# Eighteen assumed latencies of the mixers' streams raised in the driver that orders TensorE's work

## The chip, the cores and the metric

The kernel runs on one core of one Trainium2 chip. The metric is the device time of one execution in microseconds, as the median of several runs; a profiled execution beside them gives the trace. TensorE multiplies matrices, VectorE (DVE), ScalarE (ACT) and GpSimd (POOL) work on elements, SyncE (SP) issues the DMAs. The engines run side by side and wait for each other through semaphores. Each takes its own instructions in order.

## What is computed

A decoder block on 16 learned meta tokens and 512 tokens of width 1024: three token mixers in parallel, a gated merge, and a convolutional feed-forward net.

```python
h = rmsnorm(z)
p = h @ w_in                                  # 1024 x 8464: GLA, HGRN2, gates, RWKV-7
y_gla, y_hg = chunked gated linear attention  # chunks of 32, a state per head
y_rw = RWKV-7: S_t = S_{t-1} (diag(w_t) - kk_t^T (a_t kk_t)) + v_t^T k_t
z = z + (sum of sigmoid(gate_b) * (y_b @ w_out_b)) @ w_out
u = rmsnorm(z) @ w_up
z = z + (silu(conv(u)[:, :2816]) * conv(u)[:, 2816:]) @ w_down
return rmsnorm(z)[16:]
```

## The kernel before

The big products (GEMMs) are made in float16 with a high and a low part of both operands, three matmuls for one, and read their weights from HBM in blocks of 128 columns: a DMA brings a block (`wf`), ScalarE makes the high part and VectorE the low part (`split_w`, L202 and L203, tile `w`). Each such block is an *item*: 48 matmuls for a block of 1024 rows, 24 for one of 512. The items before the feed-forward net are the columns of `w_in` (one for each of q, k, v, f, g of a head or a pair of heads, and 24 gates) and the products with `w_out_*`. An item ends with the evacuation of its PSUM bank (`then`).

The mixers work on these columns in *streams*, Python generators: in the first drive four HGRN2 heads (`hg0` to `hg3`) and two pairs of GLA heads (`gl0`, `gl1`), index 0 to 5; in the second drive RWKV-7, four pairs of heads in `rw_phase1`, then the inversion of the chunks' triangular matrices on VectorE and GpSimd (`invert`, L1194 and L1199), then four pairs in `rw_phase2`. The steps of a stream are small matmuls and transposes in float32, named by their PSUM tile:

- `lin_mixer`: `pk`, `pmt`, `pv` transpose k and v; `ps0` and `pin` make the states; `pc` the scores; `po` and `pom` the outputs; `pt` transposes them back.
- `rw_phase1`: `psu`, `psa` (low rank parts), `pss` and `prb`, `prm` (norm of kk and its broadcast), `pM`, `pMm` (the matrices that are inverted).
- `rw_phase2`: `pQ`, `pN`, `tA`, `tB`, `tK`, `tV`, `tm`, `psb`, `psx`, then, with the inverse, `p1`, `p2`, `pw`, `ph`, `pf`, then the chain over eight chunks (`pc`, with latency `ch` between two chunks), and `pyt`.

Each `yield latency, banks` in a stream tells the driver how long after the step before it the next one's operands are expected, and how many of the four small PSUM banks must be free by its own account. The latencies stand in the table `LT`. `drive` fixes TensorE's order by hand when the kernel is built: it keeps a modelled clock `pe.t` (`Paced`), takes a step of a stream as soon as the clock has passed its due time, enough banks are counted free and the stream owes no filler (`owed`: after a step some filler, 0.7 of its time), and otherwise issues matmuls of the items, the *filler*. It is the order alone that is fixed so; on the chip each matmul waits for its operands. The other engines' order is made by the scheduler of the framework.

Gates: a stream can yield a name and waits for that event (`at(name, latency)`); an item can too, and then holds all items behind it. The f item of HGRN2 head 2 waits for `hg0`, the end of head 0's stream; the k item of RWKV pair 2 waits for `a0`, the end of pair 0's phase 1, that of pair 3 for `a1`. `T`, the inverse, is assumed 53.8 us after `a3`. Phase 2 of a pair waits for the r item of that pair, and that of pair 3 for `y0`, the end of pair 0. The chunk chains wait for `out27`, the end of the last product of HGRN2's output. The last items before the merge (`rw_item`) need `y0` to `y3`; the first of them takes three of its k blocks for two output blocks (36 of 48 matmuls) ahead of `y3`.

Of the kernel before, what the change touches and what calls it, by code (L numbers as in the profile page):

```python
# [18 lines left out]
P = 128  # L19
# [4 lines left out]
T = NMETA + SEQ  # L24
# [24 lines left out]
LT = dict(  # L49
    f=17.0, pk=(1.0, 1.89, 0.0, 0.0, 1.0, 0.0), pv=0.0, ps0=1.2, pc=0.75,  # L50
    po=(4.08, 2.75, 0.98, 0.0, 0.0, 2.0), pt=(10.56, 10.58, 9.41, 18.52, 18.27, 9.18), gk=0.75, v=0.0,
    gv=4.09, k=4.31, pss=(1.14, 1.4, 0.28, 1.69), prb=(2.37, 3.25, 2.02, 2.9),
    pM=(2.7, 3.05, 4.48, 2.95), pMm=0.0, r=18.93, rv=0.9, g=1.82, T=53.8, pN=0.0, tA=2.44, tB=0.0, tK=0.8,
    tm=3.44, psb=1.1, psx=1.06, p1=11.9, p2=3.06, pw=5.19, ph=0.44, pf=0.1, ch0=0.0, ch=3.4, gn=3.11, y=9.68,
    hold=1.85, mix=0.7,
)
# [38 lines left out]
def trunk(ctx: ExitStack, tc: tile.TileContext, d: dict, out: bass.AP):  # L95
# [143 lines left out]
    with tc.tile_pool(name="xin", bufs=1, side="right") as xp:  # L239
# [13 lines left out]
        pt = bank("mix_ps", P, KD)  # L253
# [111 lines left out]
    pt = bank("par_ps", P, npar)  # L365
# [216 lines left out]
    def lin_mixer(im, gev, nm, gsum, gscale, q, k, vs, sgs, normw, ys):  # L582
# [52 lines left out]
        pk = bank(f"pk{nm}", P, 4, P)  # L635
# [11 lines left out]
        for h in range(nh):  # L647
            yield LT["pv"], 1
            pv = bank(f"pv{nm}{h}", P, 4, P)
            for t in range(4):  # L650
                pe.transpose(pv[:, t, :], vs[h][:, 16 + P * t : 16 + P * (t + 1)], ident)
            v_ = lt.tile([P, 4, P], F32, tag=f"vt{h}", name=f"vt{nm}{h}")
            act.activation(v_, pv, AF.Copy)
            vt.append(v_)


        S = lt.tile([P, 4, P], F32, tag="S", name=f"S{nm}")
        yield LT["ps0"], 2
        ps0 = bank(f"ps0{nm}", P, P)
# [11 lines left out]

        yield LT["pc"], 2
        stv = []
# [3 lines left out]
        pcs = [bank(f"pc{nm}{h}", P, 4, P) for h in range(nh)]  # L677
# [333 lines left out]
    def rw_phase1(i):  # L1011
# [95 lines left out]
        for h, pq in enumerate(pqs):  # L1107
            vec.tensor_copy(Mt[:, :, h, :], pq)
        yield LT["pMm"], 2
        pms = [bank(f"pMm{i}{h}", 16, 16) for h in range(2)]  # L1110
# [119 lines left out]
    def rw_phase2(i, r1, E0, ANs, Xs, HVs, s2, s2m, s3):  # L1230
# [58 lines left out]
        for h, (pq, hr) in enumerate(zip(pqs, hrs)):  # L1289
            for q, (rr, sr_) in enumerate(par):  # L1290
                vec.tensor_tensor(X[rr, :, h, rr], pq[rr, 4 * q : 4 * q + 4, :], mU[rr], op=ALU.mult)
                vec.tensor_tensor(E[sr_, q:8:2, h, rr], pq[sr_, 4 * q : 4 * q + 4, :], mU[sr_], op=ALU.mult)
        yield LT["pN"], 2
        pns = [bank(f"pN{i}{h}", P, 4, 64) for h in range(2)]
# [7 lines left out]
        for h, (pn, hr) in enumerate(zip(pns, hrs)):  # L1302
            for q, (rr, sr_) in enumerate(par):
                vec.tensor_tensor(AN[rr, :, h, sr_], pn[rr], mL[rr], op=ALU.mult)
        yield LT["tA"], 1
        pa = tok4(f"tA{i}", Ap, 0)
# [3 lines left out]
        for h, hr in enumerate(hrs):  # L1310
            for q, (rr, sr_) in enumerate(par):
# [116 lines left out]
        yield LT["ch0"], 1

# [383 lines left out]
```

## Time and profile before

| | us |
|---|---|
| median of 3 runs | 1027.21 |
| lowest and highest run | 1023.19, 1027.33 |
| the profiled execution | 1026.22 |
| span of the profiled execution, first to last instruction | 1023.9 |

| stretch of the span, us | what runs |
|---|---|
| 0 to 250.7 | prologue, and drive 1: HGRN2 and GLA streams among their items |
| 250.7 to 324.1 | phase 1 of RWKV-7 |
| 324.1 to 443 | inversion, and phase 2 of pairs 0 to 2 up to the chunk chains |
| 443 to 578.3 | chunk chains of all pairs, phase 2 of pair 3 |
| 578.3 to 615.3 | last gates and products of RWKV-7's output |
| 615.3 to 1023.9 | product with `w_out`, feed-forward net, final norm |

In the profile PE is TensorE's matmuls and PEld its weight loads. A wait is idle time of an engine that a semaphore ended; the name behind the arrow is who set it. PEclk is the clock that TensorE was granted, as a share of 2.4 GHz; 0.50 is 1.2 GHz. A row of a window gives its bounds and length, the busy time of PE, PEld, DVE, ACT and POOL with their counts of instructions, PEclk, the busy share of the DMA engines, and GB/s. `g` is the PSUM tile of the GEMMs, `g<-hT,w` a matmul of an item of `w_in`, `g<-y,w` one of `w_out_*`. The names of tiles leave numbers out, so that `pinhg` is `pin` of an HGRN2 head and `pM` that of any pair.

### The profile page before, as it was taken

How to read it: one execution, taken by the hardware profiler on the slowest of the kernel's cores; microseconds unless marked ns; L12 is line 12 of the kernel's file. 1: busy time of each engine (PE TensorE's matmuls, PEld its weight loads, DVE VectorE, ACT ScalarE, POOL GpSimd, SP SyncE). 2: the span in 40 equal slices, each digit the busy share in tenths (PEclk: the TensorE clock that was granted, in tenths of full speed). 3: DMA queues.
4: the chain of work that ended last, by engine and by line, in shares of the span. 5: the costliest groups of instructions: out<-in, count | busy, mean ns of one | idle time of the engine just before them, and what ended most of it. 6: DMA issues, size and time to landing. Idle time of an engine off the chain costs nothing.

```text
span 1023.9 us, 20898 instructions
## 1 busy us (share of the span) xinstructions
PE 984.7 (96%) x8694; PEld 775.6 (76%) x8694; DVE 638.2 (62%) x1234; ACT 467.1 (46%) x882; POOL 140.4 (14%) x307
## 2 busy tenths in 40 slices
PE   8999989999999989999999989999999999999996
PEld 7888877887778868788878874488888888854442
DVE  5677655445677998677644485567777677783211
ACT  6767565435654444344433353553334443552100
POOL 3122211201333511111000123000000000000100
PEclk9999999999999999999999999999999999999999
DMA  6322222233224314122233463023333333472100
GB/s 192 106 69 58 63 63 83 63 94 81 84 70 115 91 46 126 39 67 63 59 87 84 126 226 106 1 84 104 104 92 96 102 104 104 146 229 99 42 14 28
DMA packets 149289, 92.35 MB, mean 90 GB/s; under 512 B 17664, under 2 KB 142073, under 8 KB 149195
## 3 DMA queue, kind: packets, MB, share of 16 engines
q1 hardware_dynamic: 149195, 91.02, 31.3%
q8 instruction: 68, 1.11, 0.5%
q14 instruction: 26, 0.21, 0.1%
HBM read 86.92 MB, written 3.95 MB: 89 GB/s over the span
## 4 chain that ended last, share of the span: by engine, by line
PE 72%; DVE 12%; ACT 7%; DMA 3%; issue 3%; POOL 2%; SPq 0%; POOLq 0%; DVEq 0%; ACTq 0%
PE g L70 56%; PE dn L70 6%; DVE w L203 2%; DVE AN L1199 1%; DVE HV L1194 1%; DMA wf<-in_w_out_dram 1%; PE pc L70 1%; ACT w L202 1%; PE pf L70 1%; PE hT L75 1%; PE pw L70 1%; PE pogl L70 1%; ACT L383 1%; DMA z<-in_x_dram 1%; PE pcgl L70 0%
## 5 line engine op out<-in xcount | busy, mean ns | idle before, releaser
L70 PEld LDWEIGHTS <-w 128*128 128x128 f16 x5856 | 570.2, 99 | 89.4 <-issue 9.2
L70 PE MATMUL g<-hT,w 128*128 128x256 f16 (+3 forms) x5280 | 620.5, 274 | 2.6 <-ACT siluhg L383 2.2
L203 DVE SCALAR_TENSOR_TENSOR w<-wf,w 128x1024 f16<-128x1024 f32 (+1 forms) x131 | 150.7, 1151 | 93.8 <-ACT w L202 93.5
L202 ACT ACTIVATE w<-wf 128x1024 f16<-128x1024 f32 (+1 forms) x131 | 130.6, 999 | 108.0 <-PE g L70 96.1
L70 PEld LDWEIGHTS <-hid 128*128 128x128 f16 x528 | 51.7, 98 | 63.0 <-issue 1.1
L70 PE MATMUL g<-y,w 128*128 128x258 f16 x576 | 75.3, 273 | 3.5 <-DVE y L447 2.0
L1691 DVE SCALAR_TENSOR_TENSOR c<-u,parB,c 128x512 f32<-128x512 f32 x88 | 66.1, 751 | 2.4
L70 PE MATMUL g<-wd,hid 128*128 128x512 f16 x264 | 57.3, 379 | 0.8 <-DVE z L1742 0.8
L70 PE MATMUL dn<-wd,hid 128*128 128x512 f16 x264 | 57.1, 379 | 0.0
L1746 POOL TENSOR_SCALAR ssf<-ssf 128x1 f32<-128x1 f32 x4 | 2.2, 540 | 311.2 <-ACT sq L1744 311.1
L70 PE MATMUL g<-woh,mT 128*128 128x512 f16 x128 | 38.9, 379 | 0.6 <-DVE z L1645 0.6
L1709 ACT ACTIVATE c<-c 128x512 f32<-128x512 f32 x22 | 13.9, 630 | 53.8 <-DVE c L1691 53.8
L1744 ACT ACTIVATE sq<-z 128x512 f32<-128x512 f32 x8 | 5.0, 628 | 72.3 <-DVE z L1742 72.3
L70 PEld LDWEIGHTS <-mT 128*128 128x128 f16 x192 | 18.5, 98 | 24.2 <-issue 2.9
L1725 DVE SCALAR_TENSOR_TENSOR wd<-wf,wd 128x1024 f16<-128x1024 f32 x22 | 26.9, 1224 | 15.6 <-ACT wd L1724 15.4
L1724 ACT ACTIVATE wd<-wf 128x1024 f16<-128x1024 f32 x22 | 23.3, 1057 | 25.1 <-DMA wf<-in_w_down_dram 25.1
L1443 POOL TENSOR_TENSOR gv<-gv,mhalf 128x2 f32<-128x2 f32 (+1 forms) x16 | 13.9, 876 | 136.2 <-DVE gv L1442 136.2
L1742 DVE SCALAR_TENSOR_TENSOR z<-g,z 128x512 f32<-128x512 f32 x4 | 2.8, 692 | 45.8 <-PE g L70 45.8
L383 ACT ACTIVATE u<-g 128x258 f32<-128x258 f32 x88 | 29.2, 373 | 0.0
L1474 ACT ACTIVATE HV<-pc 64x128 f32<-64x128 f32 x32 | 8.4, 272 | 42.8 <-DVE HV L1473 39.4
L70 PE MATMUL g<-wol,mT 128*128 128x512 f16 x64 | 24.3, 379 | 0.0
L1689 DVE TENSOR_SCALAR c<-u,parB 128x512 f32<-128x512 f32 x44 | 23.8, 542 | 0.0
(484 smaller groups left out, 1195.6 us busy)
## 6 DMA issues: line engine op xcount, KB each, us to landing
wf<-in_w_in_dram SPq DMA_DIRECT2D x65, 512.0 KB
wf<-in_w_up_dram SPq DMA_DIRECT2D x44, 512.0 KB
wf<-in_w_down_dram SPq DMA_DIRECT2D x22, 512.0 KB
wf<-in_w_out_dram SPq DMA_DIRECT2D x8, 512.0 KB
xt<-in_x_dram SPq DMA_DIRECT2D x4, 512.0 KB
wf<-in_w_out_hg_dram SPq DMA_DIRECT2D x8, 256.0 KB
wf<-in_w_out_gla_dram SPq DMA_DIRECT2D x8, 256.0 KB
wf<-in_w_out_rw_dram SPq DMA_DIRECT2D x8, 256.0 KB
```

Source lines behind the costliest of these rows:

```text
L70: r = self.eng.matmul(out, lhsT=lhsT, rhs=rhs, **kw)
L75: r = self.eng.transpose(out, in_, ident)
L202: act.activation(wh[:, :kt, :m], wf[:, :kt, :m], AF.Copy, scale=WS)
L203: vec.scalar_tensor_tensor(wl[:, :kt, :m], wf[:, :kt, :m], WS, wh[:, :kt, :m], ALU.mult, ALU.subtract)
L383: act.activation(dst[:m, off + c0 : off + c0 + n], src, func, **kw)
L1194: eng.tensor_tensor(u, bc(mats[:, j, j + 1 : n], c1 - c0), Ti[:, j, c0:c1].unsqueeze(1).broadcast_to([cnt, r, c1 - c0]), op=ALU.mult)
L1443: gps.tensor_tensor(var, var, mhalf[:, 0 : 2 * n].rearrange("p (a b) -> p a b", b=2), op=ALU.pow)
L1689: vec.tensor_scalar(c, u[:, 0:SEQ], colB(52 + j), colB(8 + j), ALU.mult, ALU.add)
L1691: vec.scalar_tensor_tensor(c, u[:, t : t + SEQ], colB(52 + 44 * t + j), c, ALU.mult, ALU.add)
L1709: act.activation(cg, cg, AF.Silu)
L1724: act.activation(wd[f][:, 0], wf, AF.Copy, scale=WS)
L1725: vec.scalar_tensor_tensor(wd[f][:, 1], wf, WS, wd[f][:, 0], ALU.mult, ALU.subtract)
```

## The change

The entries of `LT` that were one number for all heads or pairs become tuples with a number for each, and the `yield`s read them by index (`[im]` in `lin_mixer`, `[i]` in RWKV-7). Eighteen of the numbers are raised; the others stay. Nothing else changes: no instruction is added or taken away, the order in which `drive` puts them is made anew from the table. The diff, with the raised entries and two of the yields:

```diff
 LT = dict(
-    f=17.0, pk=(1.0, 1.89, 0.0, 0.0, 1.0, 0.0), pv=0.0, ps0=1.2, pc=0.75,
-    po=(4.08, 2.75, 0.98, 0.0, 0.0, 2.0), pt=(10.56, 10.58, 9.41, 18.52, 18.27, 9.18), gk=0.75, v=0.0,
-    gv=4.09, k=4.31, pss=(1.14, 1.4, 0.28, 1.69), prb=(2.37, 3.25, 2.02, 2.9),
-    pM=(2.7, 3.05, 4.48, 2.95), pMm=0.0, r=18.93, rv=0.9, g=1.82, T=53.8, pN=0.0, tA=2.44, tB=0.0, tK=0.8,
-    tm=3.44, psb=1.1, psx=1.06, p1=11.9, p2=3.06, pw=5.19, ph=0.44, pf=0.1, ch0=0.0, ch=3.4, gn=3.11, y=9.68,
-    hold=1.85, mix=0.7,
+    pk=(2.6, 1.89, 0.0, 0.0, 1.0, 0.0),
...
+    ps0=(1.2, 1.87, 1.2, 1.2, 3.96, 1.58),
+    pc=(0.75, 0.75, 0.75, 0.75, 1.57, 0.75),
+    po=(4.08, 2.75, 0.98, 1.7, 0.0, 2.0),
...
+    pss=(2.38, 1.4, 0.28, 1.69),
+    prb=(4.27, 4.12, 3.18, 3.37),
...
+    tA=(5.4, 3.11, 2.44, 2.44),
...
+    tK=(0.8, 1.29, 0.8, 0.8),
...
+    psb=(3.13, 1.1, 1.1, 1.1),
+    psx=(1.06, 1.06, 1.63, 1.06),
...
+    pw=(5.19, 6.5, 5.19, 5.19),
...
+    ch=(3.4, 3.4, 4.02, 3.4),
...
-        yield LT["ps0"], 2
+        yield LT["ps0"][im], 2
...
-                yield LT["ch"], 0
+                yield LT["ch"][i], 0
```

`ch` also sets how long the bank of the chunk chain is counted as taken, `hold=8 * (LT["ch"][i] + 0.5)`.

## Rows read from the trace of the kernel before

**Rows 1.** The page: engines' busy us; costliest groups; one window (core, engines' busy, PEclk).

```profile
PE 984.7 (96%) x8694; PEld 775.6 (76%) x8694; DVE 638.2 (62%) x1234; ACT 467.1 (46%) x882; POOL 140.4 (14%) x307
...
L203 DVE SCALAR_TENSOR_TENSOR w<-wf,w 128x1024 f16<-128x1024 f32 (+1 forms) x131 | 150.7, 1151 | 93.8 <-ACT w L202 93.5
...
443.00:578.30 135.30, 132.36 (x1381) 115.64 (x1380) 79.75 (x207) 54.24 (x126) 14.14 (x17) 1.00 0.27 74
```

**Rows 2.** Waits of TensorE: line waited for: us in total, times, longest.

```profile
PE tA L75 <- issue: 2.7, 1, 2.7
...
PE pingl L70 <- ACT vtgl L653: 2.5, 1, 2.5
...
PE psb L70 <- DVE Nm L1351: 1.8, 1, 1.8
...
PE pohg L70 <- DVE st L697: 1.5, 1, 1.5
...
PE prm L75 <- POOL rnm L1072: 1.4, 3, 0.6
...
PE pkhg L75 <- DVE k6hg L622: 1.4, 1, 1.4
...
PE pss L70 <- issue: 1.0, 1, 1.0
...
PE prb L75 <- ACT rnx L1069: 1.0, 1, 1.0
...
PE prb L75 <- DVE Mt L1108: 0.9, 1, 0.9
...
PE pw L70 <- ACT AN L1308: 0.8, 1, 0.8
...
PE ps0hg L70 <- DVE mthg L645: 0.4, 1, 0.4
...
PE tA L75 <- DVE ARBK L1292: 0.4, 1, 0.4
```

**Rows 3.** Windows after two waits, and one of 40 us: engines' busy, PEclk, DMA.

```profile
178.03:184.18 6.15, 6.15 (x38) 4.55 (x38) 2.05 (x6) 4.76 (x6) 1.15 (x7) 0.50 0.32 88
...
365.34:368.50 3.16, 3.16 (x15) 2.45 (x16) 3.06 (x9) 1.64 (x3) 0.00 (x0) 0.50 0.07 22
...
330.00:370.00 40.00, 37.28 (x359) 31.89 (x357) 39.66 (x112) 18.07 (x42) 20.33 (x44) 0.96 0.32 88
```

**Rows 4.** Timeline, VectorE and TensorE, at gate `hg0`: start, us, instruction.

```profile
70.13 0.82 DVE L729 TENSOR_TENSOR ohg<-ohg,rshg 128x640 f32<-128x640 f32 x1
...
74.48 0.66 PE L75 MATMUL pthg<-ident,ohg 128*128 128x128 f32 x4
```

**Rows 5.** Timeline, TensorE, before gate `a0`.

```profile
269.31 0.61 PE L70 MATMUL g<-hT,w 128*128 128x272 f16 x4
...
272.08 0.23 PE L75 MATMUL prm<-ident,rnm 16*128 16x16 f32 x1 [0.50 <-POOL rnm L1072]
...
272.24 2.87 PE L70 MATMUL g<-hT,w 128*128 128x272 f16 x24
...
275.05 0.69 PE L70 MATMUL pM<-ARBK 64*64 64x64 f32 x32
...
275.67 1.41 PE L70 MATMUL g<-hT,w 128*128 128x272 f16 x11
...
277.02 0.22 PE L70 MATMUL pMm<-ARBK,BKm 64*16 64x16 f32 x4
```

**Rows 6.** Timeline, the DMA queue and TensorE, at the inverse's load.

```profile
389.83 1.81 SPq L1369 DMA_DIRECT2D TT<-s  x4
...
396.77 0.60 PE L70 MATMUL p<-TT,Mt 32*32 32x32 f32 x26
```

**Rows 7.** Timeline, VectorE and TensorE, at the end of the streams.

```profile
581.88 0.42 DVE L1460 TENSOR_TENSOR y<-ARBK,y 128x256 f16<-128x256 f32 x1
...
584.16 5.49 PE L70 MATMUL g<-y,w 128*128 128x258 f16 x48
```

More of the change, by code (lines that the diff above doesn't have):

```diff
@@ L49 @@
 LT = dict(
-    f=17.0, pk=(1.0, 1.89, 0.0, 0.0, 1.0, 0.0), pv=0.0, ps0=1.2, pc=0.75,
-    po=(4.08, 2.75, 0.98, 0.0, 0.0, 2.0), pt=(10.56, 10.58, 9.41, 18.52, 18.27, 9.18), gk=0.75, v=0.0,
-    gv=4.09, k=4.31, pss=(1.14, 1.4, 0.28, 1.69), prb=(2.37, 3.25, 2.02, 2.9),
-    pM=(2.7, 3.05, 4.48, 2.95), pMm=0.0, r=18.93, rv=0.9, g=1.82, T=53.8, pN=0.0, tA=2.44, tB=0.0, tK=0.8,
-    tm=3.44, psb=1.1, psx=1.06, p1=11.9, p2=3.06, pw=5.19, ph=0.44, pf=0.1, ch0=0.0, ch=3.4, gn=3.11, y=9.68,
-    hold=1.85, mix=0.7,
+    f=17.0,
+    pk=(2.6, 1.89, 0.0, 0.0, 1.0, 0.0),
+    pv=(0.0, 0.0, 0.0, 0.0, 0.0, 0.0),
+    ps0=(1.2, 1.87, 1.2, 1.2, 3.96, 1.58),
+    pc=(0.75, 0.75, 0.75, 0.75, 1.57, 0.75),
+    po=(4.08, 2.75, 0.98, 1.7, 0.0, 2.0),
+    pt=(10.56, 10.58, 9.41, 18.52, 18.27, 9.18),
+    gk=0.75,
+    v=0.0,
+    gv=4.09,
+    k=4.31,
+    pss=(2.38, 1.4, 0.28, 1.69),
+    prb=(4.27, 4.12, 3.18, 3.37),
+    pM=(2.7, 3.05, 4.48, 2.95),
+    pMm=(0.0, 0.0, 0.0, 0.0),
+    r=18.93,
+    rv=0.9,
+    g=1.82,
+    T=53.8,
+    pN=(0.0, 0.0, 0.0, 0.0),
+    tA=(5.4, 3.11, 2.44, 2.44),
+    tB=(0.0, 0.0, 0.0, 0.0),
+    tK=(0.8, 1.29, 0.8, 0.8),
+    tm=(3.44, 3.44, 3.44, 3.44),
+    psb=(3.13, 1.1, 1.1, 1.1),
+    psx=(1.06, 1.06, 1.63, 1.06),
+    p1=(11.9, 11.9, 11.9, 11.9),
+    p2=(3.06, 3.06, 3.06, 3.06),
+    pw=(5.19, 6.5, 5.19, 5.19),
+    ph=(0.44, 0.44, 0.44, 0.44),
+    pf=(0.1, 0.1, 0.1, 0.1),
+    ch0=(0.0, 0.0, 0.0, 0.0),
+    ch=(3.4, 3.4, 4.02, 3.4),
+    gn=(3.11, 3.11, 3.11, 3.11),
+    y=9.68,
+    hold=1.85,
+    mix=0.7,
 )
@@ L647, in lin_mixer @@
         for h in range(nh):
-            yield LT["pv"], 1
+            yield LT["pv"][im], 1
             pv = bank(f"pv{nm}{h}", P, 4, P)
@@ L669, in lin_mixer @@
             vec.scalar_tensor_tensor(S[:, t + 1], S[:, t], DT[:, t : t + 1], pin[:, t, :], ALU.mult, ALU.add)
-        yield LT["pc"], 2
+        yield LT["pc"][im], 2
         stv = []
@@ L1108, in rw_phase1 @@
             vec.tensor_copy(Mt[:, :, h, :], pq)
-        yield LT["pMm"], 2
+        yield LT["pMm"][i], 2
         pms = [bank(f"pMm{i}{h}", 16, 16) for h in range(2)]
@@ L1292, in rw_phase2 @@
                 vec.tensor_tensor(E[sr_, q:8:2, h, rr], pq[sr_, 4 * q : 4 * q + 4, :], mU[sr_], op=ALU.mult)
-        yield LT["pN"], 2
+        yield LT["pN"][i], 2
         pns = [bank(f"pN{i}{h}", P, 4, 64) for h in range(2)]
@@ L1304, in rw_phase2 @@
                 vec.tensor_tensor(AN[rr, :, h, sr_], pn[rr], mL[rr], op=ALU.mult)
-        yield LT["tA"], 1
+        yield LT["tA"][i], 1
         pa = tok4(f"tA{i}", Ap, 0)
@@ L1315, in rw_phase2 @@
                 )
-        yield LT["tB"], 1
+        yield LT["tB"][i], 1
         pb = tok4(f"tB{i}", Bd, 16)
@@ L1319, in rw_phase2 @@
             act.activation(X[rr, :, :, kc], pb[rr], AF.Copy)
-        yield LT["tK"], 1
+        yield LT["tK"][i], 1
         pk = tok4(f"tK{i}", Kd, 16)
@@ L1332, in rw_phase2 @@
             act.activation(HV[sr_, q:8:2, :, :], pv[sr_], AF.Copy)
-        yield LT["tm"], 2
+        yield LT["tm"][i], 2
         pm = bank(f"tm{i}", 16, 3, P)
@@ L1351, in rw_phase2 @@
             vec.tensor_tensor(Nm[:, h, :], pm[:, 4:20], maskL[0:16, 0:16], op=ALU.mult)
-        yield LT["psb"], 2
+        yield LT["psb"][i], 2
         rw_bonus(i)
         yield "g"
-        yield LT["psx"], 2
+        yield LT["psx"][i], 2
         lg = sv[:, 0:NY]
@@ L1373, in rw_phase2 @@
         sp.dma_start(TTm, s2m[2 * i : 2 * i + 2].rearrange("h i c -> i h c"))
-        yield LT["p1"], 2
+        yield LT["p1"][i], 2
         p1 = bank(f"p1_{i}", P, 8, 32)
@@ L1387, in rw_phase2 @@
         vec.tensor_copy(Xm, pw)
-        yield LT["p2"], 2
+        yield LT["p2"][i], 2
         p2 = bank(f"p2_{i}", P, 8, 32)
@@ L1398, in rw_phase2 @@
         vec.tensor_tensor(Em, Em, pf, op=ALU.add)
-        yield LT["pw"], 2
+        yield LT["pw"][i], 2
         for t2 in range(2):
@@ L1407, in rw_phase2 @@
             act.activation(X[:, 2 * t2 : 2 * t2 + 2].rearrange("p t h n -> p (t h) n"), pw, AF.Copy)
-        yield LT["ph"], 2
+        yield LT["ph"][i], 2
         ph = bank(f"phm{i}", 64, 2, 64)
@@ L1416, in rw_phase2 @@
         for t2 in range(2):
-            yield LT["pf"], 2
+            yield LT["pf"][i], 2
             pfs = [bank(f"pf{i}{t2}{q}", P, 4, P, hold=2.0) for q in range(2)]
@@ L1427, in rw_phase2 @@
         yield "out27"
-        yield LT["ch0"], 1
+        yield LT["ch0"][i], 1
         Y = HV[:, 0:9:2]
@@ L1462, in rw_phase2 @@
         nb = 2 if i >= CH2 else 1
-        pcs = [bank(f"pc{i}{l}", P, 8 // (3 - nb), 64, hold=8 * (LT["ch"] + 0.5)) for l in range(nb)]
+        pcs = [bank(f"pc{i}{l}", P, 8 // (3 - nb), 64, hold=8 * (LT["ch"][i] + 0.5)) for l in range(nb)]
         for c in range(8):
@@ L1486, in rw_phase2 @@
             if c < 7:
-                yield LT["ch"], 0
+                yield LT["ch"][i], 0
             if c == 6:
                 finish(0)
-        yield LT["gn"], 1
+        yield LT["gn"][i], 1
         finish(1)
```

## Prediction

> **What bounds the kernel now.** I read five views, each for one question. The page's first part [rows 1] says which engine sets the time: TensorE is busy 984.7 of 1023.9 us, so 39 us of idle time and the stretches at a lowered clock are all that a change of order can win; no instruction is added or removed. The list of waits on TensorE [rows 2] says who owns this idle time: the twelve groups shown are steps of the mixers' streams and add up to 15.8 us. They are steps whose assumed latency is raised; four raised steps with less to wait are left out of the rows and of the sum. Not among them, and untouched, are the waits of plain GEMM work, such as 2.2 us for a silu's evacuation. The windows behind the longest waits [rows 3] say what an idle stretch costs after it has ended. The timelines around three gates of the order [rows 4 to 6] say whether filler is there to put in front of a step. The last timeline [rows 7] says whether the streams or the filler end the mixers.
>
> **How a raise works.** The driver takes a stream's step once its modelled clock has passed the due time, and issues filler matmuls (GEMMs on weights) until then. A latency that is too short puts the step in front of filler that could have run; TensorE is in order, so it idles. A raise by the wait plus 0.24 us puts that much filler ahead: the step starts when its operand is ready, as before, and the filler is done sooner. So a raise costs nothing where filler is at hand and something else ends last, and wins nothing where the filler is used up. The eighteen raises add up to 22.2 us (the one on `ch` counted once).
>
> **Drive 1 (GLA and HGRN2, to 250.7 us).** `pk` of head 0 waited 1.4 us, `ps0` of head 1 0.4 us [rows 2]. The f item of head 2 is behind the event `hg0`, set by the `pt` transposes of head 0: until these have run, filler ends. They started at 74.48 us, and their operand was ready at 70.95 (70.13 + 0.82) [rows 4], so they can come earlier by both waits, 1.8 us, without a wait of their own: bounds 0 and 1.8, I take 1.6. `po` of head 3, 1.5 us: the next gate is events away, so 1.4. `pin` of GLA pair 0 waited 2.5 us for ScalarE's copy of v; behind it TensorE ran 6.15 us at half of its granted clock (0.50, 1.2 GHz) [rows 3], which gives back up to 3.1 us: bounds 0 and 5.6; with 2.76 us of filler in front the wait should fall to little, I take 5.0. `pc` of that pair is raised too, by 0.82, without a wait in the list; it only moves filler: 0.
>
> **Phase 1 of RWKV-7 (250.7 to 324 us).** `pss`, `prb` and `prm` of pair 0 waited 1.0, 1.0 and 0.5 us (0.5 of the 1.4 in the row of `prm`). Here filler is short: the k item of pair 2 yields to `a0`, which pair 0 sets after `pMm`. The filler between `prm` and that gate is 24 + 11 matmuls and the last 9 of the k item of pair 1 (48 less the four that ran before them) [rows 5], 5.0 us. Of these 3.1 us (27) now go ahead of the steps; 17, 1.9 us, are left to cover the 2.8 us from `prm` to `pM` [rows 5], and nothing lies between `pM` and `pMm` any more. So the gate opens after about 272.3 + 2.8 + 0.9 = 276.0 us, and the k item of pair 2 starts some 2.2 us before the 278.2 of now (277.24 and the nine). Bounds 0 and 2.5, I take 2.0. The other waits of `prm` (0.9) and the `prb` of pair 2 (0.9, for a PSUM bank that VectorE's copy of Mt frees) meet the same kind of gate at `a1`; a bank that is late is not due time: I take 0.6 of 1.8.
>
> **Phase 2 to the event `out27` (324 to 443 us).** `tA` 2.7 and 0.4, `psb` 1.8, `pw` 0.8: 5.7 us; after the `tA` of pair 0 another 3.16 us at clock 0.50 [rows 3], worth 1.6. In this stretch VectorE is full: 39.66 of 40 us [rows 3], with the inversion of all pairs on it. Filler that is put ahead brings its own VectorE work in front of the steps' operands. The raises put 2.96 + 2.03 + 0.67 + 0.49 = 6.2 us of filler there. An item of 48 matmuls takes 5.49 us [rows 7] and costs VectorE at least one split of 1.15 us [rows 1], 0.21 us for each us of filler; at most 0.59, the share of VectorE in the stretch from 443 us, where filler and streams are together (79.75 of 135.3) [rows 1]. That is 1.3 to 3.6 us given back; I take the middle, 2.4, and 5.7 + 1.6 - 2.4 = 4.9.
>
> **From `out27` on (443 to 615 us).** The raises on `psx` and `ch` of pair 2 answer waits among the four left out: 0. The raise on `ch` acts at seven steps, 7 x 0.62 = 4.3 us on pair 2's stream, but pair 3 starts on `y0`, not on pair 2. The chunk chains of pairs 0 and 1 start at the event `out27`, which is set by filler; so everything behind it moves with the filler won before. The end is covered: y of pair 3 is ready at 582.30 us, and the first matmul that needs it is the 37th of 48 that start at 584.16, at 588.3 [rows 7]: 6.0 us of cover. The rest of the kernel from 615 us keeps its order.
>
> **New waits.** Filler used sooner means that steps meet their operands sooner. Nearest is `p1` of pair 0, which reads the inverse that four DMAs bring, issued from 389.83 over 1.81 us; it started at 396.77 without a wait [rows 6]. When they landed these rows do not tell, so `p1` could wait for all that TensorE comes sooner there, 4.9 us; but its due time follows `psx` and moves later with the raises of `tA` and `psb`. Bounds 0 and 4.9, I take 1.5, nearer to none, because 5 us lie between the last issue and `p1`. For all others, which I cannot see before they appear, 2.0 (bounds 0 and 8, half of the waits won).
>
> **Sum.** 1.6 + 1.4 + 5.0 + 2.0 + 0.6 + 4.9 = 15.5, less 3.5, is 12.0 us. The profiled execution took 1026.2 us (span 1023.9 and 2.3 around it): 1014.2. The median of the runs lies 1.0 us above the profiled one: 1015.2, and I say 1015.
>
> **Rivals.** *(a) The wait moves one step on.* Each stream is a chain of latencies, and where the filler runs out at a gate (`hg0`, `a0`, `a1`) or VectorE is the limit, the next step waits what the first no longer does. Then phases 1 and 2 win only the 1.6 us of clock, drive 1 its 1.4 + 5.0, and 2 us are lost: 1026.2 - 6.0 + 1.0 = 1021. For it: VectorE full at 330 to 370. Against it: most gaps lie behind 5 us and more of filler. *(b) The change does not do what it says.* The due time is not what holds a step: a step can also be held by a count of free banks and by the filler owed, and the engines other than TensorE are ordered anew by the scheduler, so a raise from one trace is out of date once the order has changed. The gains of some 15 us are met by as many new waits: 1026, no change. For it: the bank waits of `prb` and `psb`. *(c) Slower: the filler's own work in front of the streams' operands.* VectorE and ScalarE work their queues in order. The 22.2 us of filler put ahead bring 0.59 us of VectorE's and 0.40 us of ScalarE's time (54.24 of 135.3) for each us [rows 1], 13.1 + 8.9 = 22.0 us; if all of it fell in front of operands, it would take more than the 15.8 + 4.7 = 20.5 us of waits and clock. From there each further new wait like that of `pin` that lowers the clock adds 3.1; with two, 1026.2 + 1.5 + 6.2 + 1.0 = 1034.9. For it: both long waits were ended by ScalarE or VectorE while these were busy. Against it: other steps have slack, as `pt` with 3.5 us [rows 4].
>
> [...]
>
> **How the numbers follow.** The forecast has 0.62, (a) 0.20, (b) 0.10, (c) 0.08. A measurement of this kernel tells about 0.5% (5.1 us) from no change, so the line lies at 1022.1. The forecast is faster with all its weight; of (a), around 1021, two thirds; (b) is the same; of (c) all is slower. That gives 0.75 faster, 0.17 same, 0.08 slower. The best case, every wait and all clock won, is 1027.2 - 20.5 = 1006.7. The range leaves out its end, (c) and part of (b): 1007.5 to 1024.5. Faster cases hold most of the chance, so no second range is needed.
>
> **What would show it.** Right: TensorE's list loses `pkhg`, `pohg`, `pingl`, `pss`, `tA` and `psb` or keeps them under 0.5 us; no stretch at 0.50 at GLA pair 0 and at the `tA`; `out27` and the first `pc` of pair 0 some 11 us sooner than the 443 of now; the same distance from there to the last `y`. Wrong for (a): new waits at `pM`, `p1` or `pt`, and the first `pc` no more than 6 us sooner. Wrong for (b) and (c): a list as long as now under other names; for (c) VectorE and ScalarE busy through these waits. The forecast falls if the filler blocks at `a0` or `hg0` longer than I worked out, or if the new order of ScalarE makes a wait over 2 us somewhere with a lowered clock behind it.

## The result and the profile after

| | before | after |
|---|---|---|
| median, us (15 runs of each, side by side) | 1023.47 | 1030.09 |
| lowest and highest run, us | 1020.56, 1027.33 | 1027.87, 1031.54 |
| profiled execution and its span, us | 1026.22, 1023.9 | 1028.70, 1026.4 |

The ratio of after to before is 1.0059, with a 95% interval of 1.0048 to 1.0070: the change makes the kernel 0.6% slower, where 1.2% faster was forecast. The two profiled executions differ by 2.5 us only, since that of before lay 2.7 us above the median of these runs and that of after 1.4 us below its own.

All lines of the code now stand 31 further down: L697 of before is L728 of after. The first line of the page, against [rows 1], shows TensorE with the same work:

```profile
PE 985.3 (96%) x8694; PEld 778.2 (76%) x8694; DVE 639.6 (62%) x1234; ACT 468.7 (46%) x883; POOL 134.6 (13%) x307
```

The list of TensorE's waits answers [rows 2] (line waited for: us in total, times, longest):

```profile
PE pogl L101 <- DVE st L728: 4.5, 1, 4.5
PE pyt L106 <- DVE HV L1475: 3.3, 3, 2.1
PE prb L106 <- ACT rnx L1100: 2.9, 1, 2.9
PE pN L101 <- DVE ARBK L1323: 2.3, 2, 1.2
PE pinhg L101 <- ACT vthg L684: 2.2, 1, 2.2
...
PE pM L101 <- DVE ARBK L1123: 1.7, 2, 1.0
...
PE tA L106 <- issue: 1.5, 1, 1.5
PE pQ L101 <- DVE Nm L1382: 1.3, 1, 1.3
```

The reader is to see that the names of [rows 2] are nearly all gone: `pk`, `ps0`, `po` of `hg3`, `pin` of `gl0`, `pss`, `prm`, `psb` and `pw` wait no more, and `tA` waits 1.2 us less. Each raise did what it was made for at its own step. Other steps wait in their place, most of them one or two steps further on in the same stream: `pin` of `hg0` behind `pk`, `po` of `gl0` behind `pin`, `prb` of another pair, `pQ` and `pN` in phase 2. The longest of them, 4.5 us, is longer than any of before. Two windows, behind that wait and of the 40 us of [rows 3] (bounds and length, busy time of PE, PEld, DVE, ACT, POOL, then PEclk, DMA, GB/s):

```profile
187.72:194.54 6.82, 6.82 (x40) 6.14 (x41) 0.64 (x3) 0.82 (x2) 0.00 (x0) 0.55 0.30 79
330.00:370.00 40.00, 37.87 (x377) 32.56 (x374) 39.69 (x109) 17.11 (x41) 20.47 (x45) 1.00 0.36 95
```

The lowered clock of [rows 3] has moved with the wait, from `pin` to `po` of `gl0` (0.55 over 6.82 us). VectorE is as full from 330 to 370 us as before (39.69 of 40 us). The end, against [rows 7], from the timeline:

```profile
586.00 0.43 DVE L1491 TENSOR_TENSOR y<-ARBK,y 128x256 f16<-128x256 f32 x1 [0.48 <-ACT y L1490]
...
587.14 5.05 PE L101 MATMUL g<-y,w 128*128 128x258 f16 x44
```

The last `y` and the product that reads it both come some 3 to 4 us later than before and nothing waits between them: the loss was made earlier.

### The profile page after: what moved, and what is told of

The parts are those of the page before. It is cut to its first block, busy times and chain, and to the rows that moved or that the text cites. A ratio compares the mean times of both kernels' runs of the same rounds, so it can differ in the third digit from the quotient of the medians.

```text
span 1026.4 us, 20896 instructions
## 1 busy us (share of the span) xinstructions
PE 985.3 (96%) x8694; PEld 778.2 (76%) x8694; DVE 639.6 (62%) x1234; ACT 468.7 (46%) x883; POOL 134.6 (13%) x307
## 4 chain that ended last, share of the span: by engine, by line
PE 73%; DVE 12%; ACT 8%; DMA 3%; issue 2%; POOL 1%; SPq 1%; POOLq 0%; ACTq 0%; DVEq 0%
PE g L101 56%; PE dn L101 6%; DVE w L234 2%; DMA wf<-in_w_out_dram 1%; ACT w L233 1%; DVE AN L1230 1%; DVE HV L1225 1%; PE pc L101 1%; ACT L414 1%; PE pogl L101 1%; PE pf L101 1%; PE pw L101 1%; PE pchg L101 1%; PE hT L106 1%; PE pohg L101 1%
## 5 line engine op out<-in xcount | busy, mean ns | idle before, releaser
L1755 ACT ACTIVATE wd<-wf 128x1024 f16<-128x1024 f32 x22 | 23.2, 1057 | 24.6 <-DMA wf<-in_w_down_dram 24.5
L1504 DVE COPY HV<-pc 64x128 f32<-64x128 f32 x28 | 7.9, 288 | 18.8 <-PE pc L101 13.9
```

The source lines that it names most:

```text
L1755: act.activation(wd[f][:, 0], wf, AF.Copy, scale=WS)
```

## Where the time went

Two of the new waits, from after's timelines. At `gl0`:

```profile
185.80 1.22 DVE L234 SCALAR_TENSOR_TENSOR w<-wf,w 128x1024 f16<-128x1024 f32 x1 [3.15 <-ACT w L233]
186.95 1.32 DVE L728 COPY_PREDICATED st<-maskC,pcgl 128x512 f32<-128x512 int32 x2
...
187.72 3.96 PE L101 MATMUL pogl<-vtgl,st 128*128 128x128 f32 x16 [4.52 <-DVE st L728]
```

The scores that `st` copies were done at 179.3 us. But ahead of `st` in VectorE's queue stands the low half of a weight split, which waits 3.15 us for ScalarE's half; VectorE stood idle for these 3.15 us and did not take `st` first. In before no late split stood ahead of `st`, which waited for the scores themselves:

```profile
185.32 1.34 DVE L697 COPY_PREDICATED st<-maskC,pcgl 128x512 f32<-128x512 int32 x2 [3.64 <-PE pcgl L70]
```

And at pair 2 of phase 1, in after:

```profile
293.47 0.72 ACT L1158 ACTIVATE bon<-sk,par 128x514 f32<-128x514 f32 x1 [4.16 <-DVE sk L1152]
294.20 1.28 ACT L414 ACT_TABLE_LOAD   x1
295.49 0.66 ACT L414 ACTIVATE gate<-g 128x258 f32<-128x258 f32 x2
296.04 1.06 ACT L233 ACTIVATE w<-wf 128x1024 f16<-128x1024 f32 x1
296.98 0.63 ACT L1100 ACTIVATE rnx<-rn 128x512 f32<-128x512 f32 x1
...
297.67 0.66 PE L106 MATMUL prb<-ident,rnx 128*128 128x128 f32 x4 [2.94 <-ACT rnx L1100]
```

Here a gate's table load, its evacuation and a split, all of them filler's, stand 2.8 us long ahead of `rnx`. In before the gate and the split stood ahead of `rnx` too:

```profile
293.79 0.66 ACT L383 ACTIVATE gate<-g 128x258 f32<-128x258 f32 x2 [2.75 <-PE g L70]
...
295.39 0.63 ACT L1069 ACTIVATE rnx<-rn 128x512 f32<-128x512 f32 x1
295.92 0.71 ACT L1127 ACTIVATE bon<-sk,par 128x514 f32<-128x514 f32 x1
```

What is new in after is `bon`, a step of pair 1's stream. It stood behind `rnx` and now stands ahead of the gate, where it holds ScalarE for 4.16 us until VectorE has made `sk`; the table load, the gate and the split follow only then. So the first place is rival (c) of the prediction, filler's own work in front of an operand; at the second it is filler's work behind a stream's operation that came too early in the queue. What the runs had to tell is why this came, and whether it is the whole of the loss.

## The experiments

For each kernel the table gives its ratio to before (both run side by side), and three sums over its trace: TensorE's idle time in three stages, in all from 20 us on, and the time lost to the half clock (an estimate: half of TensorE's busy time in such stretches, also from 20 us on; in before twelve matmuls of an item took 2.75 us in the stretch at 0.50, 0.229 us each, and 48 took 5.49 us at 1.00 [rows 7], 0.114 each). Two traces of before show how far the same kernel moves. A trace's span less its last two columns is 987.5 to 989.7 us for all seventeen, so these two columns account for the differences between traces to about 1 us.

| kernel | ratio, 95% interval | drive 1 | phase 1 | phase 2 | idle in all | half clock |
|---|---|---|---|---|---|---|
| before, two traces | 1 | 8.4, 8.1 | 5.3, 4.3 | 9.1, 8.9 | 28.4, 26.3 | 6.4, 8.1 |
| after | 1.0059, 1.0048 to 1.0070 | 9.3 | 5.8 | 10.3 | 30.7 | 8.2 |
| drive 1's raises | 1.0014, 0.9999 to 1.0028 | 9.3 | 4.5 | 8.2 | 27.0 | 9.6 |
| phase 1's raises | 1.0012, 0.9997 to 1.0027 | 8.0 | 5.3 | 8.9 | 26.8 | 5.1 |
| phase 2's raises | 0.9993, 0.9980 to 1.0006 | 8.0 | 5.3 | 9.5 | 28.5 | 3.4 |
| operands first | 0.9997, 0.9984 to 1.0009 | 4.9 | 5.5 | 10.5 | 25.9 | 5.1 |
| twelve raises kept | 1.0000, 0.9984 to 1.0016 | 4.8 | 6.6 | 11.3 | 27.4 | 3.4 |
| three raises more | 0.9962, 0.9949 to 0.9975 | 4.0 | 5.7 | 11.0 | 25.7 | 2.4 |
| `gl0` alone | 0.9944, 0.9930 to 0.9958 | 5.9 | 4.0 | 11.2 | 26.3 | 1.4 |
| `gl0` and its `po` | 0.9950, 0.9936 to 0.9964 | 5.2 | 4.2 | 8.5 | 22.2 | 5.1 |
| four raises more | 0.9957, 0.9941 to 0.9973 | 4.1 | 5.7 | 9.7 | 24.6 | 2.3 |
| `gl0` and `po` of `hg3` | 1.0010, 1.0001 to 1.0020 | 8.8 | 5.1 | 8.1 | 27.1 | 5.0 |
| one entry back | 1.0014, 1.0000 to 1.0029 | 6.1 | 6.0 | 10.0 | 27.4 | 6.6 |
| two entries back | 0.9965, 0.9954 to 0.9977 | 6.3 | 3.6 | 10.1 | 24.8 | 4.5 |
| `gl0` and phase 1 | 0.9942, 0.9927 to 0.9958 | 6.0 | 2.9 | 7.9 | 21.5 | 5.5 |
| `gl0` and `tA` | 0.9929, 0.9913 to 0.9945 | 6.0 | 4.0 | 7.9 | 23.0 | 0.0 |

**Each stage's raises by themselves.** The kernel before, with the raises of one stage only, and the kernel before once more:

```diff
 # drive 1 alone: pk, ps0, pc, po as in the change; phase 1 alone: pss, prb; phase 2 alone: tA, tK, psb, psx, pw, ch
 # all else at the old values
```

> The kernel before, once more, for a second trace. The profiled run of before took 1026.2 us, but the median of its 15 runs is 1023.5. If the waits of one trace are the same in every execution, the list of TensorE's waits has the same rows within 0.1 us and the same stretches of lowered clock, and the span is 1024 again; if they differ from one execution to the next, the rows of half a microsecond and the stretches of lowered clock differ, and the span is nearer to 1021.

> Only the raises of drive 1 (pk, ps0, pc, po) are kept; phase 1 and phase 2 have the latencies of before. Theory Q (the filler put ahead brings its ScalarE and VectorE work into their queues ahead of the streams' operands, so each wait comes back at a nearby step): in the trace the waits at pin of hg0 (2.2 us) and at po of gl0 (4.5 us) are there again, drive 1 wins no more than 2 us, and the time is within 3 us of before. Rival S (each group of raises wins what its waits were, and only the three together collide): about 6 us faster than before.

> Only the raises of phase 1 (pss, prb) are kept. Theory Q: the wait at prb of pair 2 grows from 0.9 to nearly 3 us behind ScalarE's rnx, and the time is 0 to 2 us above before. Rival S: 1 to 3 us faster than before.

> Only the raises of phase 2 (tA, tK, psb, psx, pw, ch) are kept. Theory Q: the waits at tA, tB, tK, pQ, pN add up to as much as before, 6 us, and the time is 1 to 4 us above before. Rival S: 4 to 5 us faster than before.

None of the three wins anything that can be told from no change, and their ratios add up to +0.2% against the change's 0.6%. In each trace the waits that its raises answer are gone and others have come: after drive 1's raises `po` of `gl0` waits 4.5 us, after phase 1's `prb` of pair 2 waits 2.9 us. Phase 2's raises, in their list of waits and the window of [rows 3]:

```profile
PE pN L101 <- DVE ARBK L1323: 3.1, 2, 1.9
...
PE pQ L101 <- DVE Nm L1382: 1.2, 1, 1.2
```

```profile
330.00:370.00 40.00, 38.79 (x386) 33.67 (x385) 39.60 (x110) 18.62 (x46) 17.18 (x34) 1.00 0.30 80
```

`tA` and `psb` no longer wait there, `pQ` and `pN` wait instead, and VectorE is busy for 39.60 of the 40 us, which suggests (no run tests it) that VectorE holds phase 2. Its raises win 0.7 us (0.07%) at best guess. So the rival that only the three groups together collide was wrong as put; the new waits come with each group. Theory Q, that filler's ScalarE and VectorE work gets in front of the operands, was next.

**Operands first.** After, with TensorE's order untouched; a copy of one element makes two pieces of filler's work wait for the operand that they stood in front of:

```diff
+if this is the split ahead of gl0's st:      vec.tensor_copy(wl[0:1, 0, 0:1], st[0:1, 0, 0:1])
 vec.scalar_tensor_tensor(wl, wf, WS, wh, ALU.mult, ALU.subtract)
+if this is the gate ahead of rnx of pair 2:  act.activation(gate[0:1, 14:15], rnx[0:1, 0, 0:1], AF.Copy)
 evac(gate, ps, LATE, AF.Sigmoid, scale=IWS)
+if this is the split behind that gate:       act.activation(wh[0:1, 0, 0:1], rnx[0:1, 0, 0:1], AF.Copy)
```

> The changed kernel with TensorE's order and all its raises untouched; only two pieces of filler's work on the other engines are put behind a stream's operand, each by a copy of one element that reads the operand first. On VectorE the low half of one weight split (1.22 us, and 3.15 us of waiting for ScalarE ahead of it) goes behind gl0's two st copies; on ScalarE a gate's table load and evacuations and the high half of the next split (3.5 us together) go behind rnx of pair 2. Theory Q (filler's work in the in-order queues ahead of the operands is what brought the waits back): the wait of 4.52 us at gl0's po falls to 0.2 to 0.8, since the second st copy can end near 184.0 where TensorE is free at 183.2; the wait of 2.94 us at prb of pair 2 falls to 0.2 to 0.6; the half clock behind gl0's po (6.8 us) goes. TensorE's idle time after the first 20 us falls from 30.7 to 24 to 26 us, the median from 1030 to 1021 to 1025 us. Rival R (the operands' own chains are that late, whatever stands in the queues): both waits stay within 0.3 us and the time within 0.2% of the changed kernel. Rival G (the time is given back later, another wait ends last): the two waits fall, but others grow by as much, and the time stays at 1028 to 1031 us.

Its timelines at the two places (the lines are numbered a little higher again):

```profile
182.95 1.33 DVE L749 COPY_PREDICATED st<-maskC,pcgl 128x512 f32<-128x512 int32 x2
...
186.19 1.23 DVE L245 SCALAR_TENSOR_TENSOR w<-wf,w 128x1024 f16<-128x1024 f32 x1 [1.73 <-ACT w L239]
...
183.72 2.44 PE L101 MATMUL pogl<-vtgl,st 128*128 128x128 f32 x16
...
288.45 0.63 ACT L1124 ACTIVATE rnx<-rn 128x512 f32<-128x512 f32 x1 [0.77 <-POOL rn L1120]
...
289.14 0.66 PE L106 MATMUL prb<-ident,rnx 128*128 128x128 f32 x4 [0.92 <-ACT rnx L1124]
```

`po` of `gl0` does not wait at all and `prb` waits 0.92 us in place of 2.94. The ratio falls from 1.0059 to 0.9997, by 6.3 us, with the same table and the same order on TensorE. That settles what made the change slower: the places of two pieces of filler's work in two in-order queues. (At `pM` of pair 2 a wait of 1.75 us came for the 2.0 won at `prb`, since VectorE's half of that split now stands further back; so most of the 6.3 us is `gl0`'s.)

**Which raise does it?** Two guesses followed: put back the raises whose own or next step had come to wait, or go on and raise the three longest new waits as well.

```diff
 # twelve raises kept: after, with
-pk[0] 2.6, ps0[4] 3.96, pc[4] 1.57, prb[2] 3.18, tA[1] 3.11, tK[1] 1.29
+pk[0] 1.0, ps0[4] 1.2,  pc[4] 0.75, prb[2] 2.02, tA[1] 2.44, tK[1] 0.8
 # three raises more: after, with
-ps0[0] 1.2, po[4] 0.0, prb[2] 3.18
+ps0[0] 3.4, po[4] 4.6, prb[2] 6.1
```

> The changed kernel with seven of the raises put back to the old values, those whose waits came back larger: pk of hg0, ps0 and pc of gl0, prb of pair 2, and tA and tK of pair 1. Left are ps0 of hg1 and gl1, po of hg3, pss of pair 0, prb of pairs 0, 1 and 3, tA of pair 0, psb, psx, pw and ch. If each raise has its own local outcome, as read from the traces so far, then the waits of the kernel before return at hg0's pk (1.36) and gl0's pin (2.52), those of hg0's pin (2.17), gl0's po (4.52), pair 2's prb (2.94) and pair 1's pN (1.02 and 1.25) go, and idle time after the first 20 us is 22 to 25 us against 26.3 to 28.4 before: median 1017 to 1020 us, 0.3 to 0.6% under the kernel before. If instead the driver's order and the queues are laid out anew by any change of the table, so that no wait can be foretold from another kernel's trace, new waits of 2 us or more turn up at other steps and the time lies anywhere from 1019 to 1030 us.

> The changed kernel with its three largest new waits added to the table in the same way: ps0 of hg0 from 1.2 to 3.4, po of gl0 from 0 to 4.6, prb of pair 2 from 3.18 to 6.1, 9.7 us of waits in all. By the premise of the change (a latency raised by its wait wins the wait) idle time falls by 9.7 us from 30.7 to about 21 and with the half clock behind gl0's po the median falls to 1016 to 1021 us. By theory Q each raise brings more of the filler's ScalarE and VectorE work ahead of the same operand, so that at least half of the 9.7 us comes back at these or the next steps: idle 26 to 31 us, median 1024 to 1031 us.

The first was a miss: 1.0000 (six entries are put back, as listed; the "seven" of the expectation is a slip). `prb` of pair 2 waits 2.93 us although its own raise is gone, so a wait need not belong to the raise of its step. The second won 0.38% on before: the three waits are gone, and with them drive 1's idle time is 4.0 us. So Q in its strict form (more filler always brings its work in front of the operand) does not hold at these steps. Of the 9.7 us raised, idle time fell by 5.0, for a new wait of 6.4 us stood at `pN`, where VectorE's masked copies of pair 1 wait 3.83 us for the transfer that still reads X.

**One pair of heads.** The same step from the other end: before with `gl0`'s two raises only, then with its `po` too; and the chase taken one wait further.

```diff
 # gl0 alone: before, with
+ps0[4] 3.96, pc[4] 1.57
 # gl0 and its po: the same, and
+po[4] 4.6
 # four raises more: three raises more, and
+pN[1] 6.4
```

> The kernel before with the two raises of gl0 alone (ps0 of gl0 from 1.2 to 3.96, pc of gl0 from 0.75 to 1.57). By the prediction on record this wins 5.0 us: 1018 us. By theory Q the wait of 2.52 us at gl0's pin comes back at its po as 4.5 us with 0.7 us at pcm, since a weight split then stands ahead of the st copies on VectorE: idle time 2 to 3 us more, with the half clock behind po in place of that behind pin; median 1024 to 1027 us.

> The same two raises of gl0, and po of gl0 raised from 0 to 4.6 with them; nothing else differs from the kernel before. If a raise only carries the wait one step on, and the chain of steps from ps0 to po has to be covered as a whole (theory N), both waits go: pin's 2.52 and po's 4.52 are under 0.6 each, idle time is 2 to 3 us under that of the kernel before, and the half clock behind them goes too (1.7 to 3.4 us): median 1017 to 1021 us. By theory Q in its strict form (more filler in TensorE's queue always puts more of its ScalarE and VectorE work ahead of the operand) po waits 2 us or more again and the median is 1022 to 1027 us.

> The kernel with the three further raises, and in the same way one more: pN of pair 1 from 0 to 6.4, its wait of 6.41 us in that kernel's trace, where VectorE's masked copies stand 3.8 us behind the transfer that reads X. Theory N: the wait falls under 1.5 us, with the half clock behind it (6.8 us, worth some 2.4): median from 1019.6 to 1012 to 1016 us, unless a later step takes it. Theory Q in its strict form: at least half of the 6.4 us comes back at pN or at the next steps of pairs 1 to 3, median 1016 to 1021 us.

`gl0`'s raises alone win 0.56%, 5.7 us: what the prediction had put down for them (5.0), and the opposite of what I expected by then. `po` waits 0.65 us there, not 4.52. Raising `po` as well adds nothing (0.9950): its trace has 4.1 us less idle time and 3.7 us more of half clock. And the wait at `pN` does not yield to its raise: in that run it stands earlier in TensorE's order, at `psx`, as the list of waits shows first for three raises more, then for four:

```profile
PE pN L101 <- DVE ARBK L1323: 7.2, 2, 6.4
```

```profile
PE psx L101 <- issue: 5.4, 1, 5.4
```

So the raises are not good or bad each by itself. Something else in drive 1's set turns `gl0`'s win into a loss. ScalarE's order at `gl0`, read from the built instructions with each of drive 1's other raises added to `gl0`'s in turn, is changed by one of them: `po` of `hg3`.

**Two raises that collide.** `gl0`'s raises with `po` of `hg3`; and after without it:

```diff
 # gl0 and po of hg3: gl0 alone, and
+po[3] 1.7
 # one entry back: after, with
-po[3] 1.7
+po[3] 0.0
```

> The kernel before with three raises: the two of gl0 (which alone gave 1018.3 us) and po of hg3 from 0 to 1.7. Theory P (the raises are not independent: po of hg3 shifts the filler under gl0, so that ScalarE holds gl1's gf and its table load where it held silugl and the weight split, and the split that stands ahead of gl0's st copies is late): hg3's po loses its wait of 1.45 us, but gl0's po waits 4.5 us again and pcm 0.7, with half clock behind it; idle time 28 to 30 us, median 1022 to 1025 us, some 5 us over gl0's raises alone. Rival S (each raise has its own local outcome): po's 1.45 us go and nothing else changes, median 1015.5 to 1017.5 us.

> The changed kernel with one of its eighteen entries put back: po of hg3 from 1.7 to 0. Theory P: hg3's po waits 1.45 us again, gl0's po falls from 4.52 to under 0.9 us, and the 6.8 us of half clock behind it go; idle time falls from 30.7 to 26.5 to 28.5 us, median from 1030 to 1022 to 1026 us. Rival S: the wait of 1.45 us comes back and gl0's stays: 1030 to 1032 us.

`gl0` alone, the timeline of ScalarE, VectorE and TensorE:

```profile
167.85 0.65 ACT L967 ACTIVATE gf<-gf 128x528 f32<-128x528 f32 x1
...
170.97 0.64 ACT L969 ACTIVATE gf<-gf 128x528 f32<-128x528 f32 x1
...
173.41 0.66 ACT L414 ACTIVATE silugl<-g 128x258 f32<-128x258 f32 x2
...
176.82 0.64 ACT L625 ACTIVATE e1gl<-d1gl 128x528 f32<-128x528 f32 x1
...
180.89 1.06 ACT L233 ACTIVATE w<-wf 128x1024 f16<-128x1024 f32 x1
...
181.98 1.23 DVE L234 SCALAR_TENSOR_TENSOR w<-wf,w 128x1024 f16<-128x1024 f32 x1 [2.37 <-ACT w L233]
183.13 1.32 DVE L728 COPY_PREDICATED st<-maskC,pcgl 128x512 f32<-128x512 int32 x2
...
183.90 2.44 PE L101 MATMUL pogl<-vtgl,st 128*128 128x128 f32 x16 [0.65 <-DVE st L728]
```

And with `po` of `hg3` raised:

```profile
169.97 0.66 ACT L414 ACTIVATE silugl<-g 128x258 f32<-128x258 f32 x2
...
171.46 0.65 ACT L967 ACTIVATE gf<-gf 128x528 f32<-128x528 f32 x1
...
176.83 0.64 ACT L969 ACTIVATE gf<-gf 128x528 f32<-128x528 f32 x1
...
181.60 0.64 ACT L625 ACTIVATE e1gl<-d1gl 128x528 f32<-128x528 f32 x1
...
185.68 1.06 ACT L233 ACTIVATE w<-wf 128x1024 f16<-128x1024 f32 x1
...
186.76 1.22 DVE L234 SCALAR_TENSOR_TENSOR w<-wf,w 128x1024 f16<-128x1024 f32 x1 [3.15 <-ACT w L233]
187.91 1.32 DVE L728 COPY_PREDICATED st<-maskC,pcgl 128x512 f32<-128x512 int32 x2
...
188.68 1.61 PE L101 MATMUL pogl<-vtgl,st 128*128 128x128 f32 x5 [4.52 <-DVE st L728]
```

The reader can follow one chain in both. The split stands ahead of `st` in both. With the raise the filler is 1.5 us further on, so that the silu's evacuation of an item comes to ScalarE in front of `gf` (the gate that the next pair, `gl1`, reads) and not behind it. `gf`'s last step is then 5.9 us later (176.83 to 170.97), with two table loads (1.28 us each) between the `gf` steps in place of one; so are `gl1`'s `d1` and `e1`, behind which the next split waits on ScalarE; the split ends 4.8 us later, and `st` and `po` with it, while TensorE is free for `po` only 0.9 us later. From 0.9944 to 1.0010, a raise that wins its own 1.45 us costs 6.8 us together with another that wins 5.7. The spans of the two traces differ by 4.8 us: 3.6 of half clock and 0.7 of idle time (drive 1 idles 2.9 us more, phase 2 3.1 less). Taken out of the change it gives back 0.45% (1.0059 to 1.0014), and `po` of `gl0` waits 0.6 us.

**The other place, and what is left.** In phase 1 ScalarE's built order, read in the same way, shows two raises of pair 0, `pss` and `prb`, that only together put `bon` of pair 1 ahead of the gate (only putting `prb` back was run). Three kernels more:

```diff
 # two entries back: one entry back, and
-prb[0] 4.27
+prb[0] 2.37
 # gl0 and phase 1: gl0 alone, and
+pss[0] 2.38, prb[1] 4.12, prb[2] 3.18, prb[3] 3.37
 # gl0 and tA: gl0 alone, and
+tA[0] 5.4
```

> The changed kernel with two of its eighteen entries put back: po of hg3 (1.7 to 0) and prb of pair 0 (4.27 to 2.37). Theory P (the loss comes from raises that are harmless alone and move the filler under another operand together): gl0's po under 0.9 us as in the run before; pair 2's prb from 2.94 to about 0.9 us, since ScalarE then holds rnx of pair 2 as in the kernel before; the wait of 1.45 us at hg3's po and about 1.5 us at pair 0's prb and prm come back. Idle time after the first 20 us 24 to 27 us, median 0.2 to 0.7% under the changed kernel with po alone put back, and 0.1 to 0.5% under the kernel before. Rival (pair 2's wait is prb of pair 2's own raise, or has another cause): it stays at 2.9 us and the median is within 0.15% of the run with po alone put back.

> The kernel before with gl0's two raises (0.9944 of the kernel before by themselves) and phase 1's raises without prb of pair 0: pss of pair 0, prb of pairs 1, 2 and 3. Theory P: the waits at pair 0's pss (0.6 to 1.0), pair 1's prm (0.64), pair 2's prb (0.91) fall under 0.3 us each, no wait over 1.2 us appears in phase 1, and the ratio to the kernel before is 0.991 to 0.994. If phase 1 gives its waits back at pM, as the runs of phase 1 alone showed 0.66 and 0.71 there, the ratio is 0.994 to 0.996.

> The kernel before with gl0's two raises and tA of pair 0 from 2.44 to 5.4, the largest single raise of phase 2. Theory P: the wait of 2.8 us at tA, and with it the half clock behind it (3.4 us, worth 1.7), go: ratio 0.990 to 0.993. Rival (phase 2's raises win nothing, since the streams' chain on VectorE ends the waits there and filler put ahead only moves the wait to psb, pQ or pN): idle time of phase 2 stays within 1 us of 11.2 and the ratio at 0.994 to 0.996.

Two entries back, the list of waits:

```profile
PE prb L106 <- ACT rnx L1100: 2.8, 1, 2.8
...
PE pogl L101 <- DVE st L728: 0.6, 1, 0.6
...
PE prb L106 <- DVE Mt L1139: 0.2, 1, 0.2
```

The 2.8 us are pair 0's now, whose raise was put back, and more than expected; pair 2's `prb` waits 0.2. The ratio is 0.9965: of eighteen raises, sixteen make the kernel 0.35% faster, and the two others make of it 0.59% slower. Phase 1's raises without the collision take 1.0 us of idle time from phase 1 (2.9 for 4.0), which the ratio doesn't show (0.9942 to 0.9944); a wait of 2.4 us at pair 0's `prb` came, where none over 1.2 was expected. `tA`'s raise with `gl0`'s is the best kernel of the study, 0.9929, 1015.88 us beside 1023.33; but its step from `gl0` alone, 1.5 us, is within the intervals, and `psx` waits 3.5 us there where `tA` and `psb` did.

## Why the prediction was wrong

The step that failed is "a raise costs nothing where filler is at hand", and with it the term of new waits, 3.5 us: filler was at hand, and what it and the streams do on ScalarE and VectorE was queued anew, so that waits of 18.8 us came for the 15.3 that went.

**Drive 1.** The term of `gl0`, 5.0, was right for that raise alone (5.7), in part by luck: in its trace drive 1 idles 2.1 to 2.4 us less than in the two of before, phase 2 idles 2.2 more, and 4.9 to 6.7 us of half clock are gone, of which only 3.1 or 1.4 stood at `pin`. The term of `po` of `hg3`, 1.4, has the wrong sign in the change: the prediction asked whether filler was at hand, and it was; it did not ask in whose way the evacuation of that filler comes some 25 us later. `pk` and `ps0` of `hg0` and `hg1`, 1.6: the waits of 1.4 and 0.4 us went, and `pin` of `hg0` waits 2.2 in their place, since ScalarE's v copy there is 3.2 us later; first before, then after:

```profile
48.11 0.60 ACT L653 ACTIVATE vthg<-pvhg 128x512 f32<-128x512 f32 x1 [0.62 <-PE pvhg L75]
```

```profile
51.26 0.58 ACT L684 ACTIVATE vthg<-pvhg 128x512 f32<-128x512 f32 x1
```

The table load, two evacuations and a split of an item that stood behind the copy in before stand ahead of it in after, a third place of the same kind. What failed here is "without a wait of their own".

**Phase 1.** The gate `a0`, 2.0: 2.5 us of waits of pair 0 went, as said (1.0 of them, at `pss`, is not there in every execution: the second trace of before has none), but `pM` waits 1.0 in after, and pair 2 lost 2.0 more than it had waited. The idle time of the phase did not fall (5.8 against 5.3 and 4.3). The filler count that was made for the gate ended at `pMm`; pair 2 lay behind it.

**Phase 2.** 4.9 was put down and 0.7 measured. The mechanism, that VectorE's full stretch gives part of it back, stood in the text; the size was wrong. What the filler brought to VectorE was priced as its share of busy time (and `pw`'s raise of 1.31 us was left out of the filler, which would have made the 2.4 given back 3.0). With the six raises idle time did not fall at all (9.5 us against 9.1 and 8.9). That VectorE's full stretch always gives the whole back is not shown: with `tA`'s raise alone beside `gl0`'s, phase 2 idles 7.9 us for 11.2.

**New waits.** The term that failed most: 3.5 us. The new waits of after add up to 18.8 us (fifteen of them, from `po` of `gl0` to 0.26 us at a `pyt`) against 15.3 us that went. The prediction had bounded them at half of the waits won.

**The clock and the base.** The 4.7 us of half clock were not won: 8.2 us in after against 6.4 and 8.1. And the sum stood on an execution of before that was 2.7 us above the median, which I had put 1 us the other way; with that put right the forecast would have been further off.

**The rivals.** (c) named the mechanism and a time, 1034.9, that is nearer to the result than the forecast, with a chance of 0.08. Its price was wrong in kind: not each microsecond of filler brings its share; nearly all of it falls harmlessly and two places hold the loss. Of the two long waits that it rests on, [rows 2] puts only `pin` down to ScalarE; at `tA` it has `issue`. The sentence in (b) that a raise from one trace is out of date once the order has changed is what happened, and deserved more than 0.10. That ScalarE and VectorE work their queues in order, on which (c) rests, agrees with the runs: VectorE idled 3.15 us at the split while `st` stood behind it, and with two pieces of work put behind the operands in these queues, 6.3 us went.

**The signs.** A list as long as before under other names, put down for (b) and (c), is what came. The first `pc` of pair 0 was a poor sign of progress: it came 7.2 us sooner (436.06 against 443.25), while the first of the next pair came 8.0 us later (451.89 against 443.92) and the last `y` 4.1 later.

**Open.** Why the raises of phase 2 move their waits to just `pQ`, `pN` and `psx` was not taken apart; that VectorE's queue makes them is read from the traces, not tested. Nor was `pin` of `hg0` tested by the order of ScalarE's queue; that a further raise removes it (three raises more) is what the runs show.

## What to carry to other kernels

Where an order is planned by hand for one engine, a wait taken from a trace is a fact about the queues of all engines under that order, and a correction from it holds for one correction at a time: make it, take a new trace, and only then make the next. Before filler is put in front of a step, follow the filler past its own engine, to its evacuations and splits in the queues of the others, and see which operands will stand behind them (here `st` behind a split that waited 3.15 us). When many small corrections together lose, put them back one by one where the queue's order changes; here two of eighteen held all of the loss.

## What the runs showed of the hardware

In these traces the half clock did not follow from the length of the wait before it. After the wait of 4.6 us at `tA` with `gl0` and phase 1, and after that of 3.5 us at `psx` with `gl0` and `tA`:

```profile
359.00:369.20 10.20, 9.05 (x47) 7.32 (x48) 9.73 (x27) 4.73 (x8) 0.00 (x0) 0.57 0.07 20
```

```profile
376.90:383.70 6.80, 6.80 (x99) 5.74 (x98) 4.99 (x17) 1.93 (x3) 1.11 (x2) 1.00 0.79 162
```

The first had a granted clock of 0.57 over 10.2 us, the second of 1.00 over 6.8 us. Nor was it the same behind one and the same wait: after the 4.5 us at `po` of `gl0` the next 6.8 us had 0.55 in after and 0.72 with `gl0` and `po` of `hg3`. After the 2.9 us at `prb` of pair 2 the next 6.8 us had 1.00, in after and with phase 1's raises. In the two traces of before the waits repeat within 0.2 us, but for four that differ by 0.6 to 1.0 (two of them stand in one trace only). The stretches behind them do not repeat: behind `pin` of `gl0` the granted clock was 0.50 over 6.15 us in one trace and 0.77 over 6.26 us in the other, which costs about 3.1 and 1.4 us (estimates, by the matmuls of 0.229 and 0.114 us above). Whether this is what spreads the runs of one kernel is not shown: they lie 1.1 and 1.4 us apart for `gl0` alone and with its `po`, and 2.1 to 8.1 us for the others, but `gl0` and `tA`, with the same waits as `gl0` alone up to 350 us, spread over 4.1 us.

The traces give the granted clock as a share. What goes with it in them is a rate: at 1.00 the 264 matmuls `dn` of 512 columns took 57.14 us in before, 0.216 us each, about 2.4 columns a ns, and at 0.50 the matmuls of an item ran half as fast as at 1.00 (0.229 us for 0.114). The figures in GHz ahead of the prediction are to be read as this rate.
